# A two-layer hybrid trunk: one wide diagonal at the start, three readerless products before it, and another written-out order

## The chip, the cores and the metric

The kernel runs on one core of a Trainium2 chip, as one program. Its time is device microseconds of one execution; of several runs the median is given. The core has five engines that run their own instruction queues and wait for each other by semaphores: TensorE (PE in the profile; PEld are its weight loads), VectorE (DVE), ScalarE (ACT), GpSimd (POOL) and SyncE (SP), which here only issues DMAs.

## The reference

The input is a sequence of 2048 frames of width 1024. Two layers are applied. Cut to what is computed:

```
for l in range(2):
    shift, scale, gate = split(silu(c) @ w_ada[l] + b_ada[l])
    h = rms_norm(x, norm_g[l]) * (1 + scale) + shift
    gq, gk, gv, glr, gz, dq, dk, dv, dz = split(h @ w_in[l])
    # group A: causal convolution and silu on gq, gk, gv, then gated
    # linear attention in chunks of 64 frames with a decaying state
    # group B: two softmax maps per head, s1 - lam * s2, block-causal
    y = concat(o_gla, o_diff) @ w_out[l]
    x = x + gate * y
```

There are four heads in each group. In group B the queries and keys are normalised, the softmax is over all earlier chunks, and the result of a head is normalised and multiplied by silu of its gate path. Everything is float32.

## The kernel before

The sequence is cut into four units of 512 frames, so there are eight (layer, unit) pairs. For each unit the kernel forms h transposed, as eight tiles of 128 features by 512 frames, each split into a rounded part `hhi` and a remainder `hlo`. A weight block is split the same way into two halves of `w`. A product of two float32 matrices is then three fast products: high by high, high by low and low by high (`mm3T`, `mm3N`). They add up in PSUM banks named `acc` or `sc`. Nine weight items belong to a layer: 0 to 3 the heads of group B, 4 and 5 the inputs of group A, 6 its gate, 7 and 8 the two halves of the output.

For a head of group B and a tile of 128 queries, `scores` forms the products `sc<-Kj,qh`, VectorE writes them negated into `s` with a running minimum, ScalarE takes the exponential, and VectorE combines the two maps. `pv` transposes the map (`tp<-ident,s`), ScalarE copies it, and the products `po<-Vt,s` and `po<-Vj,s` (plain float32, two TensorE instructions each) give the result. Then ScalarE squares it, GpSimd takes the root (`wq`) and VectorE writes `z`. Four tiles of `z` are transposed (`tp<-ident,z`) and split into `oh` and `ol`, with which the output products `acc<-oh,w` and `acc<-ol,w` run in `out_gen`: two halves of eight blocks of twelve products. Block 7 is the last head of group B, blocks 0 to 3 are group A.

The start is written apart, in `start`. It loads c (`cb`), four x tiles (`xt`), the modulation weights of the first layer in eight blocks (`wm`, 1 MB each), x transposed (`xp`) and raw weights. ScalarE sums the squares of each frame; `root` (VectorE `xms`, GpSimd `rs128`) gives the reciprocal roots, one column per 128 frames. They have to lie along the free axis in all partitions. So four VectorE instructions multiply the identity by one column each (tile `dg`, called `t` in the profile), and four products with a matrix of ones spread them over the partitions into one PSUM tile `pb` (tag `tp`). ScalarE copies that to `rsb`. For each block k, VectorE forms shift and scale with two long multiply-and-sum instructions (`wm<-wm,cb`, 1024 wide), then `sv`, `B` and `A`. `make_h` makes `xp`, `hhi` and `hlo`, and 24 products of items 0 and 4 follow.

The order of the work is not the order of this text. `Program` records every instruction (19403), with a cost from `cost` and fixed delays between engines. `order` then lets the engines run in time: each takes the ready instruction with the lowest turn. The turns come from `ORDER`, a packed list of small steps; an instruction's number plus the running sum of the steps is its turn. Written out, the turns are each number from 0 to 19402 once, so they are the place of each instruction in one long list. In the first 45 us of the trace each engine follows it. All instructions are issued from line 358, so the profile's rows are told apart by tile names, not by lines. VectorE's list at the start reads: `xms`, three diagonals, `wm`, `cact`, `wm`, `cact`, the fourth diagonal, `sv`, `B`, six small vectors and `A`, two weight remainders, `xp`.

PSUM has four `acc` buffers and four of tag `tp`, which `sc`, `tp` and `po` share. All DMAs of the kernel are issued by SyncE in list order.

Of the kernel before, what the change touches and what calls it, by code (L numbers as in the profile page):

```python
# [124 lines left out]
class Program:  # L125
# [236 lines left out]
def trunk_kernel(ctx, tc, xl, x, c, ccol, w_ada, w_mod, w_all, w_glr, w_gk, vecs, lam, out):  # L362
    nc = tc.nc
    L = w_all.shape[0]
    NU = xl.shape[0]
    S = NU * UT
# [299 lines left out]
    def start():  # L666
        y = layers[0]
# [24 lines left out]
        V.scalar_tensor_tensor(cb, th, 1.0, cb, op0=ALU.add, op1=ALU.mult)  # L692
        t8 = p_sm.tile([P, KT], F32, tag="t8", name="t8", bufs=1)
# [640 lines left out]
def _layouts(x, c, w_ada, b_ada, norm_g, w_in, conv_w, w_gk, b_gk, gla_norm_g, qn_g, kn_g, lam_q1, lam_k1, lam_q2,  # L1334
# [30 lines left out]
    'NgDTBtVkdU0o_u0@)*wP4Gg?xnTy&zm}NCo>f`bR5Lg(;GG5oe-vs`QnpHJbN;yxvO3Z=cSz0kbTu$e7FgHemw|nzPiYnA+aGqN1s(yIZGnry2LV'
    '8-y&fYT-8%wDsC4|{t8$u>hPKnfGHIALh$i!P4GA9|*9YcCj0o--_V5h?iqD(mfwsiaL#Y}ACr<%ey-W8hDK@z68EuoC-BF0ZNf!rf~)OS93VeMg'
    'v9=QKhXxN|vD1USG!i&b^#rh&)NrxX&SMq_<Fmq3~sLP;2RBcgYKR%LCKWJmzN?+IO=OPUMYZXS(0{VsX-s03uSEWIF^ztgEKWH-lAkC-5GZii*f'
    'aziIqtsqON0cO}eg%_BtF8e{=h}WJ{?z9vj$9ODd?S_(lqkB1foB5O;+q6(rjm(}_HSYC-9N$$V2~Ge^q5GL(9>9kQyr^7G~2;a>j)}q2IQ|nXB='
    'gPJ@wfFx9gfMsh9TL<IBkuf$@c*H&L1DHfaHQV8q`$gPwBuS$?1p+Gy4=F76XcMOG8g7Z4HDDLED`CzC~amx(bZxEh+j2kfsja&;cE#$bPk@R`vz'
# [24 lines left out]
    '@FGaw~vnMgEB)kcEMPA)}s>3+>^>Dz1}Oe26tS$xVR81d1L9yjRZtm7IF_|ME>(i%#XW7{F~{wR}IMQYij+|!~ux{jR&a1d}MYT)^{<mvD+Fd=7e'
# [179 lines left out]
```

## Time and profile before

| | us |
|---|---|
| runs | 2431.47, 2435.93, 2436.93 |
| median | 2435.93 |
| profiled execution, time | 2435.78 |
| profiled execution, span of the core | 2434.1 |
| TensorE busy | 2378.5 |
| VectorE busy | 1823.4 |
| ScalarE busy | 1232.5 |
| GpSimd busy | 125.7 |

The mean granted TensorE clock is 0.995 of full speed. The time is the device's, the span is from the first to the last instruction of the core. Busy shares are means over very different stages. A timeline row gives start, duration, engine, line, operation, output and inputs, shapes, the number of instructions merged into it, and in brackets the idle time of the engine just before with what ended it.

### The profile page before, as it was taken

Reading aid. Unit: us, or ns where it says so; the run is one execution under the profiler, and the core shown is the slowest. Engines: PE = TensorE matmul, PEld = TensorE weight load, DVE = VectorE, ACT = ScalarE, POOL = GpSimd, SP = SyncE. Lnnn points to the kernel's source line nnn. Section 1 sums busy time; section 2 is a strip of 40 time slices with the busy share of each in tenths; the row PEclk is TensorE's granted clock in tenths of the full one; section 3 lists DMA queues with packets and bytes.
Section 4 is the critical chain, followed back from the end, with each engine's and each line's share of the span. In section 5 each row is a group of like instructions: output and inputs, shape, how many; then the busy total and the mean of one; then the engine's idle time right before and its main releaser. Section 6 shows DMA issues by size and latency. Waiting matters only on the chain.

```text
span 2434.1 us, 38504 instructions
## 1 busy us (share of the span) xinstructions
PE 2378.5 (98%) x12895; PEld 1943.7 (80%) x12895; DVE 1823.4 (75%) x5159; ACT 1232.5 (51%) x2726; POOL 125.7 (5%) x400
## 2 busy tenths in 40 slices
PE   7999999999999999999999999999999999999998
PEld 5777787777888778888788777888787887888887
DVE  7878877896578858689965897368764888748883
ACT  3876643555245544445764565245532555324452
POOL 0010000000000000000010010000000000000000
PEclk9999999999999999999999999999999999999999
DMA  8577788786777868678557777676685777776763
GB/s 324 207 267 281 266 316 270 228 278 220 248 233 221 263 212 273 191 222 241 188 205 277 275 257 256 229 236 208 205 271 205 225 221 225 250 234 204 199 211 122
DMA packets 370101, 575.86 MB, mean 237 GB/s; under 512 B 191888, under 2 KB 251760, under 8 KB 366832
## 3 DMA queue, kind: packets, MB, share of 16 engines
q1 hardware_dynamic: 369904, 573.41, 71.4%
q8 instruction: 102, 1.67, 0.3%
q14 instruction: 95, 0.78, 0.1%
HBM read 418.13 MB, written 161.50 MB: 238 GB/s over the span
## 4 chain that ended last, share of the span: by engine, by line
PE 68%; DVE 18%; ACT 5%; DMA 5%; issue 3%; POOL 1%; SPq 0%; POOLq 0%; DVEq 0%; ACTq 0%
PE acc L358 47%; PE sc L358 10%; DVE s L358 8%; PE po L358 7%; PE tp L358 4%; DMA wr<-in_w_ada_dram 2%; DVE t L358 2%; ACT s L358 1%; DVE w L358 1%; DVE xp L358 1%; DVE vN L358 1%; DVE z L358 1%; DMA w<-wd 1%; DVE am L358 1%; DMA s<-ad 1%
## 5 line engine op out<-in xcount | busy, mean ns | idle before, releaser
L358 PE MATMUL acc<-w,hhi 128*128 128x512 f32 x2560 | 841.1, 403 | 5.4 <-ACT hhi L358 2.5
L358 PEld LDWEIGHTS acc<-w,hhi 128*128 128x128 f32 x2560 | 471.9, 189 | 104.2 <-ACT hhi L358 3.9
L358 PE MATMUL acc<-w,hlo 128*128 128x512 f32 x1280 | 497.3, 401 | 0.0
L358 ACT ACTIVATE s<-s,mx 128x128 f32<-128x128 f32 (+15 forms) x256 | 308.3, 1205 | 313.0 <-DVE s L358 188.1
L358 DVE TENSOR_SCALAR_CACHE_REDUCE s<-sc,mx 64x64 f32<-64x64 f32 (+5 forms) x640 | 305.9, 482 | 54.9 <-PE sc L358 35.9
L358 PE MATMUL acc<-oh,w 128*128 128x512 f32 x1024 | 341.8, 401 | 2.6 <-DVE z L358 1.7
L358 PE MATMUL acc<-hhi,w 128*128 128x512 f32 x960 | 315.7, 399 | 1.3 <-ACT ub L358 0.7
L358 PEld LDWEIGHTS acc<-w,hlo 128*128 128x128 f32 x1280 | 240.5, 189 | 47.5 <-DVE hlo L358 1.6
L358 PEld LDWEIGHTS acc<-oh,w 128*128 128x128 f32 x1024 | 191.1, 189 | 43.9 <-DVE z L358 3.9
L358 PEld LDWEIGHTS po<-Vj,s 128*128 128x128 f32 x1536 | 207.2, 196 | 13.8 <-DMA s<-ad 2.6
L358 PE MATMUL po<-Vj,s 128*128 128x128 f32 x1536 | 214.7, 281 | 2.7 <-DMA s<-ad 1.5
L358 PEld LDWEIGHTS acc<-hhi,w 128*128 128x128 f32 x960 | 178.5, 188 | 37.8 <-DVE z L358 1.2
L358 DVE SCALAR_TENSOR_TENSOR s<-s,r 128x512 f32<-128x512 f32 (+2 forms) x320 | 202.2, 666 | 3.1
L358 PE MATMUL acc<-ol,w 128*128 128x512 f32 x512 | 203.3, 400 | 0.0
L358 DVE TENSOR_SCALAR_CACHE_REDUCE s<-sc 128x512 f32<-128x512 f32 (+4 forms) x256 | 158.2, 620 | 55.0 <-PE sc L358 34.9
L358 PE MATMUL acc<-hlo,w 128*128 128x512 f32 x480 | 189.1, 397 | 0.0
L358 PE MATMUL sc<-Kj,qh 128*128 128x512 f32 x384 | 159.1, 417 | 2.4 <-DVE s L358 1.8
L358 PE MATMUL sc<-Kj,ql 128*128 128x512 f32 x384 | 151.6, 399 | 0.0
L358 DVE SCALAR_TENSOR_TENSOR t<-ub,vec,t 128x512 f32<-128x512 f32 x192 | 140.2, 745 | 9.6 <-ACT t L358 8.9
L358 ACT CAST w<-raw 128x512 fp32r<-128x512 f32 x160 | 98.1, 625 | 93.6 <-PE acc L358 74.4
L358 POOL MEMSET s<- 64x64 f32 x256 | 36.9, 144 | 2075.3 <-PE po L358 1309.2
L358 DVE TENSOR_TENSOR w<-raw,w 128x512 fp32r<-128x512 f32 x160 | 108.7, 685 | 33.6 <-ACT w L358 31.8
(183 smaller groups left out, 3617.1 us busy)
## 6 DMA issues: line engine op xcount, KB each, us to landing
w<-wd SPq DMA_DIRECT2D x416, 512.0 KB, 4.3
wd<-w SPq DMA_DIRECT2D x144, 512.0 KB, 5.0
raw<-in_w_all_dram SPq DMA_DIRECT2D x80, 512.0 KB, 5.3
Kj<-kd SPq DMA_DIRECT2D x48, 512.0 KB, 5.9
ad<-s SPq DMA_DIRECT2D x24, 768.0 KB, 4.7
s<-ad SPq DMA_DIRECT2D x24, 768.0 KB, 6.6
wr<-in_w_ada_dram SPq DMA_DIRECT2D x128, 128.0 KB, 4.5
ad<-s SPq DMA_DIRECT2D x32, 512.0 KB, 3.9
```

The costliest lines, as they stand in the source:

```text
L358: getattr(self.engines[e], method)(*[real(a) for a in args], **{k: real(v) for k, v in kw.items()})
```

## The change

Four parts:

- In `start`, the four diagonals become one VectorE instruction over 128 x 4 x 128 elements. Its two inputs are the identity and the four columns of roots, both broadcast. The four products become one 512 wide.
- Ahead of it, three products of the ones matrix with the first 512 columns of `cb` are recorded. Each writes a `tp` tile that nothing reads.
- In `cost`, DMA rows 1024 wide get 480 in place of 350. An instruction on up to 64 partitions and 64 elements gets 216. VectorE's fixed part becomes 81 (130 for one element) in place of 70. A branch for ScalarE instructions of one element stands behind a return for all ScalarE instructions, so it is never reached.
- `ORDER` is another list. 19400 instructions are recorded, and its turns are each number from 0 to 19399 once.

```
         if e == "S":
-            return math.prod(out.shape) * 4 / {64: 208.0, 256: 326.0}.get(out.shape[-1], 350.0)
+            return math.prod(out.shape) * 4 / {64: 208.0, 256: 326.0, D: 480.0}.get(out.shape[-1], 350.0)
...
+        if out.shape[0] <= 64 and n == 64:
+            return 216
...
         if e == "A":
             return 0.834 * n + (45 if psum else 85) + 93 * (scalars + ("accum_out" in kw)) + half
+        if e == "A" and n == 1:
+            return 100 + 93 * ("bias" in kw)
...
-        return (0.52 if fast else 1.042) * n + 70 + 61 * scalars + half + 30 * ("accum_out" in kw)
+        return (0.52 if fast else 1.042) * n + (81 if n > 1 else 130) + 61 * scalars + half + 30 * ("accum_out" in kw)
...
         V.scalar_tensor_tensor(cb, th, 1.0, cb, op0=ALU.add, op1=ALU.mult)
+        for _ in range(3):
+            T.matmul(tp(), ones, cb[:, 0:512], start=True, stop=True)
...
         pb = tp()
-        for t in range(TT):
-            ts_ = slice(t * P, (t + 1) * P)
-            V.tensor_scalar(dg[:, ts_], ident, rs128[:, t:t + 1], None, op0=ALU.mult)
-            T.matmul(pb[:, ts_], ones, dg[:, ts_], start=True, stop=True)
+        V.tensor_tensor(dg.rearrange("p (t n) -> p t n", t=TT), ident.unsqueeze(1).to_broadcast([P, TT, P]),
+                        rs128[:, 0:TT].unsqueeze(2).to_broadcast([P, TT, P]), op=ALU.mult)
+        T.matmul(pb, ones, dg, start=True, stop=True)
         rsb = rs_tile()
...
 ORDER = (
...
```

Compared place by place, 78 of 100 instructions stand within 50 places of the old one. Three parts of the new list matter below.

- VectorE at the start: `cact` twice, `xms`, `wm`, the diagonal, `sv`, `wm`, `A`, a cast of the gate weights, a weight remainder, `B`, a weight remainder, `xp`. SyncE at the start: one x tile, c, one x tile, `cact`, `vec`, two x tiles, `wm`; before, `vec` and `cact` stood behind the first `wm`.
- TensorE at the tail, from the last `po` product: three output products, a transposition of `z`, five output products, the last transposition of `z`, five output products, then block 7. All thirteen are of blocks 1, 2 and 3 of the first half. Before, it was four transpositions of `z` and then block 7.
- In the first layer, unit 0, head 3 and unit 2, head 3 have more products between the scores of a tile and its transpositions than before; unit 3, head 2 has fewer.

More of the change, by code (lines that the diff above doesn't have):

```diff
@@ L1365 @@
[L1365 to L1369, printed above, removed]
@@ new lines @@
+    '6nc)Y3woiQz#W;@rW~(ndgA7_vn(3iZxbn@^eI~4BJc($x)$4T@e2(Aat^)f@-=^%gQ@6o-7{Y4NH}(dAL-mt1m+TWVM2dn*oB8o+T$8WImaNTu9'
+    'T3iDmNEo<~7NW35)fUuYuOE2!ml%g+k98?!)G30ZP;PtoB5L0%ynDxXi6y4${y+Hy|zA@t8CI&8cshhyjyI}>Es=_WGzh3UkBjnRA4@$<ysSp-in'
+    'gYDtAcd_peLW-sAb~<1OPH_YYOsRCU1+iqMG@NhME8jT~h%dSx#q=f&Vff-&-1vJ$o%JUz`%A6x<-6i;XUXaMEK+WB2HPPjBcg*He*HK>@DOV{bX'
+    'L)U`d>_!D7kqr{-sQQg5wx%r<@z%SHFs^SN3QCTp(od#lW$fWhs_9p*`e4DocfvT<lX_N1?6M>*0ozVNdlL;=I=Nwk?L{FL~MX*rABpWknIKSu=^'
+    'ks__?b5$4HazYU$YWoV|hv(QklnpCp$RQS1*69OF~-c5|3tj+JE-|&J9Iu>yNxCa`7z`X8N;lYA(dVO*qoyuCTM>p4jf652C$`Wccn`A(3cGhD9#'
@@ new lines @@
+    'P-c^m|TGN%7=#PXrs=qUcm?qcIbHQ^B#mRW&%GNU^R6DuB2YL+#Me*osp`!S9@S#GS^mpAmZ=i;KqT|TgDsxj8=A1cz_<fCY%IjaXgvQg@_F|nGi'
+    '0ED=oLn`kgIrqR;Om7!i>q0OI?XmOM;3_Ln@fqhb=Yn;`7E5Vm(9b5*3|_UZEZi^bpG5Z%ycbw~wxZ)i+zW9yR4AwvtRyuYzs3pC7`2}e`?+<LSh'
+    'a%B<H@MrXRNau^EAJ^5u&HBBsOJMmj>ye;hLNdte7b~fQYv)8zNdKYoMXixB2OfyNiPt2jG?9=4Rqid{T55=C)D|{*Bm-yc0}VZ@rXaqe--HwL<@'
+    '&P5){cRglrufBcZ<e|WlnF9y-BZrScrLDc_4PPBl3Q($xa;q5gT8j+kS@qj}qskxx23l1|B_ghw%ints^FmyQmwy02!|d*EO?hpipkY0ul|{>zv{'
+    'xxXBk0;Ge+`SU?|)&b@3s7c?NM_H+9$lA!Ri82uW0y-gDUX0q2zhO}^UvN60|63Zr#BI0`rB`wa!Ck9MR5fbH4Yc&G~_<WDL*gl-@@no^i!B4;Tp'
@@ new lines @@
+    'yMYJRFHu&f%UIW44%r?^j?4jZa&~o-i`XlFq?7<5*NN&6Z`l-&?1G!6{~%P{lnXDNR0D^4mUdY;R1qPdF>vgjfgeh9!+~*By|QJcO3^52m<c|3DQ'
+    'yY%l19b{dbw<>Vsi;$f?CWA!WO|oCplpEK~T={h6uM6cx$?tQ@c;6;2324XeeFHzamgZU4|zVMEj;#k-ayILW2Ml7_Blt+uEu42PP*28Q6I*Yx2$'
+    'Ab2Fbb4J0R3<PYQDS1`Ak)+yO`NHOZ6N-<SkF=5i7z`T5oQVkb`>AV^j9~9f32o9EEDzEAceB@zhDH$;fGa)0%p%)Dr-Lz2Y6cr-XM<e;xc9*~Dl'
+    'n<(M>>Iq+zfcOxf1?~Th(bQkAyHo4JKymxskp3Zp_UBsa}g^H$)LeT{+yRcKx)*J#PtJSPrr@gbk`&c;9tK?o4JOYu^}P`Woh&kTVms8-jiCm;NX'
+    '(Jc>J))6Hl7HkIaG)WvabRe{`TdzOW_%e`+s>U)$b)-axSi{iKX(n{*VM#X}+yI({gyA55_f(ded?~}Kmv~<WsI>a8meJ5k`g(q^>-U@MIcdrT{u'
@@ new lines @@
+    '6@3<GSw;l8_fdCH$W*az45-Y^|M^4bN#6lRtB=pauUlr_nXpVt^nZG&&-EHpxPKB6LDcGco4K-OlX@V$CfjhZj7$deAZ2Y>7ARFohxs{_<b5I<fN'
+    'Kn3ftY3OZC}FiR=y8TjdP9a{_cW8u6CUcm2m2lYj?xUo{-0`tlUHU>A>?TXKQUt}+poFLTbbf{GG;TD72ZvP93$9g@o91#Q8}sSd{O&7{y+5iEzJ'
+    'nv+}84|uFtY&z?LVmwOfgfpiSrXzwHC0y;yTGR0)ikIrR<R0WPzif19al`PxpgTffAhf2r!eq+=N`2}<mARTB83@Fs2J%=P&qyQd-mOEHk`pjS>9'
+    'VGnvS)t?!KGS@(W-CkF}q;FpH50vp~%&X2CM1(%$ZJ`HSPnE><6WjVGinQqn&E^;F5wQT7<e{ib%bfASlj~X@>Jd*yO|xCoClH?F~u@DkOLjwEeX'
+    '+(2l0>$rYP`z^%w8q8QdYWY`1gIb)lsD<|t0YWW#L7ANL2evfznr#J}WPD=Yitqlvr^Wy6`-7Ywp;((CrvGi+zCi2ngES2!E1#Rq=b&H#d#j=V8n'
@@ new lines @@
+    '`VS!9A58{hA&%3udVQMrXAWHv~o_9UZ)-@RJkc~7AN=MZpE=CKlsUJ2^2xi5a$MX9<)}9dpZN{nG_>lM~9rvLmvrRSBBs=RQ8~~i4rl-m9?8}E6O'
+    '^!jrNWw0Fk{-Qt=xxOw1Az6R!kFL_WO@N?N8_Fn=sLq5u7R{V&Y+O1G*jT_}rzcR=Ea`LxN>shn6JpfwqcZep{;F10l=XX#O9_d6Ddxv4ALdhxFv'
+    '=#w!P8iwk8gPUb|va;1@gmv)E5Yj6TK4b8|o$Jj^8`sdH2wSi>sa_xvBDItVp~x&JLi4&|JAE2*OgRITf~UD#M6=3B+0W?sS<Ok0MqrKlQE>&V6D'
+    'u_VKH%Hp&UbQ4FYxOzL@f1(4cMi<()o;ejNOTrQ!=?GBa$WYd;s-LV2ZU;ljPgdXU8AJfGXMkTvs9c!;hC);uRT(MQ^^AITe#Il%*X?1ISYL#H1c'
+    'GP4f!9jr?R9<*7;<aw6O-VZ(AY^>=G6BIF+AC}#*XXIg_ips5R-I>|!|a!4W(cg`NO<5{H94d<%8Wc}9y>HBep+r^4oap_#-rVwO{Bpm-${*#~+W'
@@ new lines @@
+    '}LTC0Ct4p;+R|yGmL7`qV<a(kx{o|1!KVhW^XTIk>niFqHX8UZf&c@6IdM-B&C{mTJiO(e$&xt&>E*+<*zJmjsv3d5qn6Xr8pbkechVvZ#_*s%z-'
+    'g8IXutA)$TgVD;AnL%X~?Pl%#>%bYV1~tksbs<TttQu5hCcNnmpz?nAI6X=|T{39idFkkj;IT~Wl&<M$;|n+vj?ey;|%po5()=fA!XeWd!Zd1zqB'
+    'W{Ry`{}E}FdGS;<LVm}hbpzlDVrNjo6oVk)rzAPL!cI=na|G34fVQR~Og%{k_TVEJwoyFMa5`Fi3^3KOp8zc<cArXHx*@0~b};m9p6h1Uy7%P_>;'
+    '}4vO41R0l*+t8-u9KnG0>KKAqHM;DvkM}Fg>bAZOC|bEiCqtg$y*uU*4eO<7LNURhQ=4p>xBC^U;)TrF@fXkB^C!Cy6YpvkFSw$_fQhrK3cp#9X)'
+    '}f*{zqP0HDL>jIzVbn~e|$V8T&uz3>qgd)<V1ol!gC35MYs?qJPhCV1bQOn9jQqg9VjYsxq${JM}*e<a<FcvkwS4za8p;heLOM*tXPY92+X7s)Q4'
@@ new lines @@
+    'iQ-IeHPF;Z(}$AIc)`|@!j16!S6;ba}9Zt*T|exmXB!xGO+xQi!ZscbP2k~+m<mDk${VxQehtz<C|c;n&bi*5F9W;z<K7Kx9n}FBSs>bSa~g;$9&'
+    'B8Ph+|aQ%ZW3or@|7ymK8|?q{De-@{(ii7Tn?2Ys*;<7`Ebb|pqQX2E#as6OM+t-L%ZMsV%5K~*!B-@g3#k9SQocbsE{^~%3EI;bl-vH-mLb#lRH'
+    '(*&=I*}mi5f83vD!;kT+V10sU*{f$KzL&7Kk#vB~vmq_teN`o){h1~X9t4dU5x_QWSteQLez7+kaeL7c-SY7T4^Lc`fR|=weWYAlEW!9SWUu_<AN'
+    'oi2kbz*}GP`CynhhjbegYZ3KK!f4{tds6w3#W^a+ms~om_@g2=%Yr`v9>YQKvgHu9Li=hcrmjuvx0X>{{c|YFvHUY_vl=^Pqior&a|w9ikV3DDl1'
+    'rkbGh|vFZ8j>DZ{CKNDj>0vCRvd`-43gVPW;UE8?5TJ?sf^t9XK3gH?PD|egK#eX9{%jkWQGa${B81D?&N?18B`h+^r?B>O6tqb-iI5J<_+Ak^?m'
@@ L1552 @@
+    'Iz_iqjlCOJPe*nwaIxCR8n(ZSYukDX{^#F`bKkTG`Ol>q+IhJaIs(kN@#Az8c_D?2rwb>hAHi}(g=PU<I0(6PRn{!vMwp|v^DYWsSr|xXsh{`EbP'
+    'd|LOntxluFrxw-L@F<Pg&E6#CJ4To;S?s+>YwJ|bEmo*g5z9C0f>&`^1z?GsM(L;pRj)U#G_)-Gy+j5OJG%i*Iehe*dnAjpVe6nl_bqXNEWrvr^A'
+    '{=OxRxy?W>4^@e2U(2JDb{=KMrK!N~<B(g_30c@2n1wi}uQjztNQ`RtCX)<z$FT~Br0cgKV3ckv00000jjZC?5lq&<00Fs-0g$f(Y}L33vBYQl0s'
+    'sI200dcD'
 )
```

350 lines of the change are left out of this document (163 added, 187 removed).

## The prediction

> **What bounds the kernel now.** I read the page first: the busy shares, then the chain that ended last.
>
> ```profile
> span 2434.1 us, 38504 instructions
> PE 2378.5 (98%) x12895; PEld 1943.7 (80%) x12895; DVE 1823.4 (75%) x5159; ACT 1232.5 (51%) x2726; POOL 125.7 (5%) x400
> ...
> PE 68%; DVE 18%; ACT 5%; DMA 5%; issue 3%; POOL 1%; SPq 0%; POOLq 0%; DVEq 0%; ACTq 0%
> ```
>
> TensorE is idle for only 2434.1 - 2378.5 = 55.6 us, and it is two thirds of the chain. The change takes no real work from it. So the time can move in three ways only: TensorE starts its stream earlier or later, its idle spells grow or shrink, or it runs for more or less time at half clock. The profiled execution took 2435.78 us by the times, 0.15 us under the median 2435.93, so a sum made against it stands for the median. Its span is 1.7 us shorter than its time, and I keep that difference.
>
> Next I read the timeline of the start and the busy table of the stages where the granted clock is below 1.00 (columns after the stage: TensorE, its weight loads, VectorE, ScalarE, GpSimd, granted clock, DMA share, GB/s).
>
> ```profile
> 7.71 1.22 DVE L358 SCALAR_TENSOR_TENSOR cb<-th,cb 128x1024 f32<-128x1024 f32 x1 [5.06 <-ACT th L358]
> 10.60 1.06 ACT L358 ACTIVATE xt<-xt 128x1024 f32<-128x1024 f32 x1
> 11.78 0.17 DVE L358 TENSOR_SCALAR xms<-xss 128x4 f32<-128x4 f32 x1 [2.84 <-ACT xt L358]
> 12.03 1.03 POOL L358 TENSOR_TENSOR rs<-xms,mhalf 128x4 f32<-128x4 f32 x1 [10.32 <-DVE xms L358]
> 13.09 0.68 DVE L358 TENSOR_SCALAR t<-ident,rs 128x128 f32<-128x128 f32 x3 [1.15 <-POOL rs L358]
> 13.44 1.22 PE L358 MATMUL tp<-t,ones 128*128 128x128 f32 x4 [13.44 <-DVE t L358]
> 13.69 1.22 DVE L358 SCALAR_TENSOR_TENSOR wm<-wm,cb 128x1024 f32<-128x1024 f32 x1
> 16.13 0.28 DVE L358 TENSOR_SCALAR t<-ident,rs 128x128 f32<-128x128 f32 x1
> 17.72 0.58 ACT L358 COPY rsb<-tp 128x512 f32<-128x512 f32 x1 [0.62 <-PE tp L358]
> 18.34 0.75 DVE L358 SCALAR_TENSOR_TENSOR xp<-xp,A,rsb 128x512 f32<-128x512 f32 x1
> 20.02 2.08 PE L358 MATMUL acc<-w,hhi 128*128 128x512 f32 x4 [2.33 <-ACT hhi L358]
> 24.02 1.05 PE L358 MATMUL acc<-w,hhi 128*128 128x512 f32 x2
> 24.88 0.63 PE L358 MATMUL acc<-w,hlo 128*128 128x512 f32 x1
> 26.60 0.85 PE L358 MATMUL sc<-hhi,w 128*128 128x512 f32 x3
> 27.29 0.39 PE L358 MATMUL sc<-hlo,w 128*128 128x512 f32 x1
> ```
>
> ```profile
> 20.00:60.00 40.00, 39.98 (x165) 32.74 (x166) 37.29 (x86) 12.55 (x20) 0.67 (x5) 1.00 0.80 315
> 104.00:108.00 4.00, 3.17 (x12) 1.95 (x10) 3.84 (x15) 2.25 (x8) 1.01 (x3) 0.52 0.65 227
> 220.00:240.00 20.00, 16.51 (x81) 12.34 (x81) 19.17 (x76) 14.63 (x43) 2.60 (x10) 0.93 0.89 323
> 240.00:260.00 20.00, 19.82 (x90) 14.98 (x89) 20.00 (x40) 10.68 (x20) 0.73 (x2) 0.90 0.42 149
> 860.00:880.00 20.00, 17.46 (x100) 14.46 (x99) 16.86 (x54) 12.42 (x35) 1.67 (x7) 0.91 0.74 208
> 2400.00:2420.00 20.00, 17.70 (x76) 14.25 (x75) 4.10 (x6) 1.35 (x4) 0.54 (x1) 0.91 0.54 189
> ```
>
> Two things are to be seen. The first 128x512 products start 0.43 us apart ((24.88-24.02)/2) and from 26.60 on 0.23 us apart ((27.29-26.60)/3), so TensorE runs its first six microseconds at half speed. And from 20 to 60 us both TensorE (39.98 of 40) and VectorE (37.29 of 40) are nearly full. Half speed returns at three later places and at the tail.
>
> **The tail.** In the timeline after the last attention block TensorE has nothing left but the chain of that block:
>
> ```profile
> 2399.66 1.06 PE L358 MATMUL po<-Vt,s 128*128 128x128 f32 x8
> 2402.56 0.33 PE L358 MATMUL tp<-ident,z 128*128 128x128 f32 x1 [1.52 <-DVE z L358]
> 2403.67 1.22 PE L358 MATMUL acc<-oh,w 128*128 128x512 f32 x4 [0.78 <-ACT oh L358]
> 2405.11 0.63 PE L358 MATMUL acc<-oh,w 128*128 128x512 f32 x1
> 2405.54 0.63 PE L358 MATMUL acc<-ol,w 128*128 128x512 f32 x1
> 2411.83 0.39 PE L358 MATMUL acc<-ol,w 128*128 128x512 f32 x1
> 2412.06 0.61 PE L358 MATMUL acc<-oh,w 128*128 128x512 f32 x2
> 2412.51 0.39 PE L358 MATMUL acc<-ol,w 128*128 128x512 f32 x1
> ```
>
> It waits 1.52 and 0.78 us and then runs at 0.43 us a product (2405.11 to 2405.54) instead of 0.227 ((2412.51-2411.83)/3). The old order leaves only three transpositions behind the last po product. The new order leaves products of the first half of the output (its blocks 1, 2 and 3): 8 of them and one transposition before the last z transposition, 5 more before the first product that needs its result. The chain from the end of po (2399.66 + 1.06 = 2400.72) to 2402.56 takes 1.84 us; the cover is 8 x 0.227 + 0.11 = 1.92 us. The next link, 2402.56 to 2403.67, takes 1.11 us; the cover is 5 x 0.227 = 1.13 us. Both just reach. So 2.30 us of waits go, and with them the half clock: (1 - 0.91) x 20 = 1.8 us, all of it lost time, since TensorE has work without a break from 2403.67 on. **Term: -4.1 us.** Bounds: 0 if the held products are missed where they stood before, -4.1 otherwise. I take the full value, since the attention rows before it are covered by transpositions and po products in both orders.
>
> **The start.** The three readerless products read cb, which is complete at 7.71 + 1.22 = 8.93 us. No such fp32 128x512 product is in the trace. The 128-wide pairs bound it: eight po instructions (four products) span 1.06 us at full clock, so a four times wider product is about 1 us; at half speed it is about 1.8 us. Three take 3 to 5.4 us, until 12 to 14.3 us. TensorE is idle until 13.44 now, and its next product must wait for the diagonal, so they cost nothing unless that product were ready before 14.3.
>
> The diagonal is one 128x512 VectorE instruction in place of four of 128x128 (0.28 us each, 0.23 apart in the row of three). The nearest row is another 128x512 two-operand instruction without PSUM:
>
> ```profile
> L358 DVE TENSOR_TENSOR w<-raw,w 128x512 fp32r<-128x512 f32 x160 | 108.7, 685 | 33.6 <-ACT w L358 31.8 <-DMA wd<-w 0.9
> ```
>
> 0.69 us against 4 x 0.23 = 0.92: 0.2 us less, bounds 0.5 less to 0.5 more for the two broadcast inputs. One wide product instead of four narrow ones is equal work. What matters is place. Before, the fourth diagonal stands behind two modulation products and runs at 16.13, so rsb is ready at 18.30 and xp starts at 18.34: the root ends last. In the new order one modulation product (1.22 us) stands ahead of the whole diagonal and the other behind it. The loads of vec and cact now go ahead of the third and fourth x load; they are 74 KB against 512 KB for each x load, whose squares follow each other every 1.3 us, so xms moves from 11.78 to about 12.0. The first modulation weights land about two such loads later (1 MB), near 13.4; then 1.22 us of product, 0.69 us of diagonal: 15.3. The wide product and the copy (0.58) make rsb ready at 17 to 17.8. But VectorE then has the second modulation product, the vector A, a gate weight cast and two weight remainders (0.69 each) ahead of xp: 15.3 + 1.22 + 0.3 + 0.25 + 1.38 + 0.1 = 18.5. So xp starts at 18.5 against 18.34 and the first product at about 20.1 against 20.02. The wait moves from the root to VectorE. Bounds: 1.7 us earlier (xp right behind A) to 1.8 later (the gate weights' VectorE work of about that size is now ahead of the first products). **Term: 0.**
>
> Does the clock stay up? Here idle time of only 1.67 us was followed by half speed:
>
> ```profile
> 103.74 0.41 PE L358 MATMUL tp<-ident,s 128*128 128x128 f32 x2 [1.67 <-DVE s L358]
> ```
>
> and the row 104 to 108 grants 0.52. Between the wide product's end (about 16.5 to 17.2) and 20.1 lie about 3 us, so I expect the first products cold again. The Trainium skill's "TensorE: Matmul & The Clock Gate", in its Part 1, says otherwise: a window of about 3.4 us of activity releases the clock and a whole idle window of that length takes it back. By that rule three products release it and 3 us would not always take it back; the sum would then gain the cold start. This is the first rival below.
>
> **The new order elsewhere.** The list gives every instruction another place, most within 50 of the old one. What I can price is TensorE work between a result and its user, counted at 0.227 us a product. At three known waits it differs much.
>
> ```profile
> 237.30 0.47 PE L358 MATMUL tp<-ident,z 128*128 128x128 f32 x1 [2.07 <-DVE z L358]
> 867.23 0.71 PE L358 MATMUL po<-Vt,s 128*128 128x128 f32 x4 [1.14 <-ACT s L358]
> ```
>
> At 237.30 (unit 0, head 3) the cover of the third z grows from 1.1 to 8.8 us, and that from the last scores to their first transposition from 1.4 to 9.9. Idle 2.07 plus clock (0.07 + 0.10) x 20 = 3.4 make 5.5 us at most. But VectorE is full there (19.17 and 20.00 of 20), so only the VectorE work that the new order puts behind counts: about 1.7 us, by the counted durations. **Term: -1.7** (0 to -5.5). At 867.23 (unit 2, head 3) the cover grows from 2.8 to 5.1 us; idle 1.14 plus (1 - 0.91) x 20 = 1.8 is 2.9 at most. VectorE has room, but a chain of about 5.4 us would still not be quite covered. **Term: -1.5** (0 to -2.9). Against it: in unit 3 of the first layer, head 2, the cover of the last tile falls from 8.1 to 4.8 us. That chain is one reduction, the exponential and four combining instructions:
>
> ```profile
> L358 ACT ACTIVATE s<-s,mx 128x2048 f32<-128x2048 f32 x16 | 32.1, 2007 | 14.8 <-DVE s L358 14.6
> L358 DVE SCALAR_TENSOR_TENSOR s<-s,r 128x512 f32<-128x512 f32 x224 | 160.5, 747 | 2.1
> ```
>
> 2.0 + 4 x 0.7 + about 1.6 = 6.4 us, so up to 1.6 us is new idle; in unit 0, head 0, one z cover falls to 1.6, below the 1.84 of the tail. **Term: +1.0** (0 to +1.9). All other waits I take as redrawn with mean 0 and about 4 us either way. The wait at 103.74 has the same instructions around it in both orders and stays. The corrected model figures cost nothing on the chip; they act only through the order.
>
> **Sum.** -4.1 + 0 - 1.7 - 1.5 + 1.0 = -6.3: 2435.8 - 6.3 = **2429.5 us**.
>
> **The rivals.**
> 1. The clock stays up through the start, or the two middle spells pay in full. A warm start is worth about 5.7 us x half = 2.8 us (20.02 to about 25.7). For it: the readerless products fill 3 us or more. Against: 3 us idle behind them, and VectorE nearly full until 60 us, so a faster TensorE only waits. The full middle spells are worth 3.8 + 1.4 = 5.2 more than I took. 2429.5 - 2.8 = 2426.7; with all, 2421.5.
> 2. The order only moves the idle spells. For it: TensorE's work is the same and the held products were filling other waits. Then only about half of the tail remains and the waits elsewhere come back: 2435.8 - 2 = 2434, within 2431.1 to 2440.
> 3. Slower: VectorE sets the pace in the first 40 us. By the counted durations the new order has 2.7 us more VectorE work ahead of TensorE's first 20 us of products (gate weights drawn forward). If TensorE then waits over about 1.5 us for the second or third h tile, a cold spell like that at 103.74 follows: 1.67 idle and about 5 us of clock (104 to 108 alone: 0.48 x 4 = 1.9). 2435.8 - 4.1 + 2.7 + 1.7 + 5 = 2441. Against it: from 20 to 48 us the chain is TensorE's own, and by 50 us of products VectorE's lead is gone.
> 4. The chip doesn't follow the list. In the trace of before it does, as far as the start and tail show, so this goes into rival 2.
>
> **Chances.** Forecast case (2426.8 to 2431.0) 0.42; rival 1 0.17; rival 2 0.27; rival 3 0.14. About 0.2% (4.9 us) is what a measurement of this kernel tells from no change. Faster by more: 0.42 + 0.17 = 0.59, less 0.01 for the edge: 0.58; within: 0.28; slower: 0.14. The range leaves out the full sum of rival 1's edge and rival 3's far part: 2420 to 2441; the likeliest case's own range is 2426 to 2433.
>
> **What would show it.** After: no wait of over 0.5 us between the last po and the last products, and granted clock 1.00 over the last 30 us; if not, the first term is wrong. One wide diagonal near 15 us behind one modulation product, xp near 18.5 and the first product near 20, spaced 0.43; spacing 0.23 at once means rival 1. Waits of TensorE in the 20 to 60 us stage mean rival 3. Clock 1.00 in 220 to 260 and 860 to 880 shows the middle terms; TensorE idle in all well under 55.6 us the whole. If idle is the same and the time too, it is rival 2.

## The result, and the profile after

The kernel after takes 2416.87 us (median of four runs, 2414.58 to 2419.43) against 2434.77 for the kernel before (2431.47 to 2436.93): a ratio of 0.9928, 95% interval [0.9911, 0.9945], or 17.9 us less. The forecast was 2429.5 within 2420 to 2441. So the direction was right and the size was about a third of what came. The profiled execution took 2415.17 us, its span is 21.0 us shorter than that of before.

The page of the kernel after, its span, busy shares and chain:

```profile
span 2413.1 us, 38502 instructions
PE 2369.6 (98%) x12895; PEld 1944.9 (81%) x12895; DVE 1825.1 (76%) x5156; ACT 1235.0 (51%) x2726; POOL 121.1 (5%) x400
...
PE 56%; DVE 4%; ACT 2%; DMA 2%; issue 1%; POOL 0%; SPq 0%; DVEq 0%; ACTq 0%; POOLq 0%
```

TensorE's busy time fell by 8.9 us although the readerless products add 5.5. To see real work alone I leave out the start. The busy table from 20 us to the end, of before and then of after (the columns after the stage are TensorE, weight loads, VectorE, ScalarE, GpSimd, granted clock, DMA share, GB/s):

```profile
20.00:2434.10 2414.10, 2376.08 (x12887) 1941.84 (x12887) 1813.76 (x5120) 1221.98 (x2709) 123.64 (x391) 1.00 0.72 236
```

```profile
20.00:2413.10 2393.10, 2362.74 (x12887) 1942.36 (x12887) 1815.40 (x5118) 1225.30 (x2711) 118.98 (x391) 1.00 0.72 238
```

The same 12887 instructions take 13.3 us less busy time, and idle time falls from 38.0 to 30.4 (2414.10 - 2376.08; 2393.10 - 2362.74). The granted clock explains part of the busy time. The stages of the kernel after that answer to those shown of before:

```profile
20.00:60.00 40.00, 38.48 (x160) 30.68 (x161) 38.84 (x90) 12.76 (x21) 0.76 (x5) 0.96 0.81 319
104.00:108.00 4.00, 2.96 (x10) 2.17 (x11) 3.81 (x17) 2.21 (x7) 0.17 (x2) 0.62 0.63 214
220.00:240.00 20.00, 16.43 (x82) 13.32 (x81) 18.83 (x70) 13.62 (x39) 2.52 (x9) 0.95 0.84 300
240.00:260.00 20.00, 19.75 (x100) 15.04 (x99) 19.84 (x44) 11.50 (x23) 0.83 (x3) 0.96 0.54 196
860.00:880.00 20.00, 18.96 (x111) 15.51 (x111) 14.78 (x50) 10.38 (x26) 1.30 (x5) 1.00 0.71 211
2400.00:2410.00 10.00, 9.42 (x41) 7.14 (x39) 2.65 (x4) 0.00 (x0) 0.00 (x0) 1.00 0.51 188
```

The dip at 860 and the one at the tail are gone (0.91 to 1.00), those at 220 and 240 are smaller, the one at 104 stays. Over all stages of 20 us the missing clock is 12.2 us before and 8.6 after. The row of before hides 2.8 us more: it grants 1.00 from 20 to 60 while the products there are 0.43 us apart until 25.7, because its trace holds no record of the clock ahead of 25.62. So 15.0 became 8.6.

The start of the kernel after, from the timeline:

```profile
9.13 1.22 DVE L362 SCALAR_TENSOR_TENSOR cb<-th,cb 128x1024 f32<-128x1024 f32 x1
10.40 5.49 PE L362 MATMUL tp<-cb,ones 128*128 128x512 f32 x6 [10.40 <-DVE cb L362]
12.44 0.17 DVE L362 TENSOR_SCALAR xms<-xss 128x4 f32<-128x4 f32 x1 [1.81 <-ACT xt L362]
13.74 1.23 DVE L362 SCALAR_TENSOR_TENSOR wm<-wm,cb 128x1024 f32<-128x1024 f32 x1 [1.14 <-DMA wm<-in_w_mod_dram]
14.89 0.69 DVE L362 TENSOR_TENSOR t<-ident,rs 128x512 f32<-128x512 f32 x1
15.68 1.34 PE L362 MATMUL tp<-t,ones 128*128 128x512 f32 x2
18.26 0.73 DVE L362 SCALAR_TENSOR_TENSOR xp<-xp,A,rsb 128x512 f32<-128x512 f32 x1
19.80 1.22 PE L362 MATMUL acc<-w,hhi 128*128 128x512 f32 x2 [2.78 <-ACT hhi L362]
20.82 1.91 PE L362 MATMUL sc<-hhi,w 128*128 128x512 f32 x4
23.22 0.62 PE L362 MATMUL sc<-hhi,w 128*128 128x512 f32 x2
28.05 0.50 PE L362 MATMUL sc<-hhi,w 128*128 128x512 f32 x1 [1.02 <-ACT hhi L362]
```

The three products take 1.8 us each, the wide diagonal 0.69, xp starts at 18.26 and the first product at 19.80, all close to the forecast. From 23.22 on products are 0.23 us apart, 2.5 us earlier than before. But at 28.05 TensorE waits 1.02 us for the next h tile, so nothing of it is left.

### The profile page after: what moved, and what is told of

Same layout as the page of the kernel before. It is cut to its first block, busy times and chain, and to the rows that moved or that the text cites. A ratio compares the mean times of both kernels' runs of the same rounds, so it can differ in the third digit from the quotient of the medians.

```text
span 2413.1 us, 38502 instructions
## 1 busy us (share of the span) xinstructions
PE 2369.6 (98%) x12895; PEld 1944.9 (81%) x12895; DVE 1825.1 (76%) x5156; ACT 1235.0 (51%) x2726; POOL 121.1 (5%) x400
## 4 chain that ended last, share of the span: by engine, by line
PE 56%; DVE 4%; ACT 2%; DMA 2%; issue 1%; POOL 0%; SPq 0%; DVEq 0%; ACTq 0%; POOLq 0%
PE acc L362 37%; PE sc L362 8%; PE po L362 7%; PE tp L362 3%; DVE s L362 2%; DMA w<-wd 1%; DVE t L362 1%; ACT la L362 0%; ACT s L362 0%; ACT L362 0%; DMA out_dram<-rt 0%; DMA xp<-xd 0%; DVE ql L362 0%; DMA wr<-in_w_ada_dram 0%; DVE w L362 0%
## 5 line engine op out<-in xcount | busy, mean ns | idle before, releaser
L362 PE MATMUL acc<-w,hlo 128*128 128x512 f32 x1280 | 490.1, 399 | 0.2 <-DVE hlo L362 0.2
L362 ACT ACTIVATE s<-s,mx 128x896 f32<-128x896 f32 (+15 forms) x256 | 308.4, 1205 | 344.0 <-DVE s L362 201.9
L362 PE MATMUL acc<-oh,w 128*128 128x512 f32 x1024 | 330.4, 396 | 1.6 <-DVE z L362 1.1
L362 DVE SCALAR_TENSOR_TENSOR s<-s,r 128x512 f32<-128x512 f32 (+3 forms) x320 | 202.6, 666 | 2.7
```

Source lines behind the costliest of these rows:

```text
L362: getattr(self.engines[e], method)(*[real(a) for a in args], **{k: real(v) for k, v in kw.items()})
```

## The experiments

In both kernels the issued order is the list itself, on each engine. So an experiment can graft one list into the other. All kernels below but the two with exchanged figures have this edit, which alone changes nothing, and a list of their own:

```
-        return self.order(turn.tolist())[0]
+        return np.argsort(turn).tolist()
```

To compare traces inside, I count TensorE's instructions from the first product of h on, each weighted by its width (transpositions and plain float32 products twice: 128 columns of them take about 0.11 us, 512 of the others 0.23), and take for each kernel the time at which it has done as much as the kernel before at a given time. The table gives the difference in us (below zero: ahead of the kernel before), one profiled execution each.

| at (us of before) | after | list only | first layer new | second layer new | tail new | old figures | TensorE swapped | VectorE, ScalarE swapped |
|---|---|---|---|---|---|---|---|---|
| 45 | 1.1 | 1.3 | 1.1 | -1.5 | -0.2 | 3.0 | 2.5 | 3.7 |
| 366 | -2.4 | -1.8 | -1.2 | -2.6 | 0.2 | -1.1 | 2.8 | 3.4 |
| 884 | -6.8 | -6.6 | -3.7 | -4.1 | -0.1 | -1.4 | 8.2 | 10.0 |
| 1197 | -8.1 | -7.1 | -4.7 | -3.5 | -0.1 | -2.0 | 7.8 | 10.2 |
| 1980 | -14.6 | -14.8 | -4.9 | -7.9 | -2.5 | -5.1 | 6.4 | 10.4 |
| 2398 | -17.1 | -16.8 | -4.7 | -10.9 | -3.2 | -5.3 | 4.9 | 10.2 |
| 2411 | -21.0 | -20.7 | -4.8 | -14.9 | -7.2 | -9.3 | 1.0 | 6.2 |

How far one curve can be read: the kernel with only a new tail has the old order until 2343 and still drifts by up to 3.1 us, and the one with the second layer new stands 4.1 us ahead at 884, where its order is still the old one. In another kernel (one transposition moved, below) a stretch of 100 us without any edit lost 2 us to the kernel after, with two waits of 0.66 and 0.35 us for weights (`DMA w<-wd`). So differences under about 4 us in this table are one execution's own.

### Where along the kernel the gain arises

**The first layer in the new order, the second in the old.** ORDER: the first 9800 places of the new list, then the old order.

> The kernel after, whose instructions follow its own list up to place 9800 (about 1197 us, the end of the first layer) and the old list's order behind it. Theory S (the gain is a sum of local waits, removed stage by stage): at equal TensorE work the kernel after stands 9.9 us ahead of the kernel before at 1197 us, so this kernel is 9.9 us faster than before (2425 us) and runs at the old pace behind. Theory W (the gain comes from the start parts, the readerless products and the wide diagonal, and all later work only starts earlier or meets other waits): the whole 18 us, 2417. Theory T (only the removed tail is real, the rest is redrawn with mean 0, as I had predicted): 0, 2435. Theory L (a list works only as a whole): less than 4 us, over 2431.

Measured: 2427.24, ratio 0.9975 [0.9965, 0.9986], 6.1 us faster. **The second layer in the new order**, on the kernel before with its own start:

> The kernel before with its own start (four narrow diagonals, no readerless products) and its old list up to about 1197 us, and the new list's order behind it. Theory S: the second layer with the tail accounts for what is left of the whole, 18 to 21 minus 9.9, so 8 to 11 us faster than before (2424 to 2427). Theory W: 0 (2435). Theory T: the tail alone, 4.1 us (2431). Theory L: less than 4 us.

Measured: 2423.45, ratio 0.9958 [0.9945, 0.9970], 10.2 us faster. The two halves together make 16.3 of the 17.9 us. W falls: a kernel with the old start has most of the gain. T falls: the tail cannot be 10 us. S holds in sum, though the first layer gave less than its 9.9 (the table has 8.1 there for the kernel after).

**The tail alone.**

> The kernel before with its old list up to about 2343 us and the new list's order only in the last 3 per cent. My prediction's first term: 4.1 us faster (2430.7), no wait of over 0.5 us between the last po product and the last products, granted clock 1.00 over the last 30 us. Theory S by the aligned traces: 4 to 5 us. Theory W: 0. Theory T: 4.1.

Measured: 2430.03, ratio 0.9992 [0.9983, 1.0002]: 1.9 us, with an interval from 4.1 faster to 0.5 slower. In its trace there is no TensorE wait over 0.5 us after 2353.5, and from 2398 to 2411 it gains 4.0 us in the table. The kernels after, list only, and both with swapped queues gain 3.9 to 4.0 there too. The trace shows the term of 4.1; the times of this one kernel don't confirm it.

**The list alone**, without the wide diagonal and the readerless products:

> The kernel before with its own instructions (four narrow diagonals in one row where the wide one stands, four narrow products, no readerless products) in the new list's order throughout. Theory S: the list is all of it, and at the first product the two kernels stand within 0.2 us, so 16 to 18 us faster than before (2417 to 2419), within 2 us of the kernel after. Theory W: 0 to 4 us (the tail). The first 20 products then show the old spacing of 0.43 us until about 2.8 us later than in the kernel after.

Measured: 2418.73, ratio 0.9942 [0.9928, 0.9956], 14.1 us faster. The interval meets that of the kernel after: the other parts are worth between nothing and some 3 us.

**The kernel after without its readerless products:**

```
-        for _ in range(3):
-            T.matmul(tp(), ones, cb[:, 0:512], start=True, stop=True)
```

> The kernel after without its three readerless products (nothing reads what is left out); all else in the same order. Theory S, and my prediction's start term of 0: the first products are spaced 0.43 us until about 2.8 us later than in the kernel after (25.7 instead of about 23), but the kernel after waits for the next h tiles there anyway, so from 45 us on the two stand level and the time is that of the kernel after (2417, within 2 us). Theory W2 (the earlier end of the half clock is worth its 2.8 us to the end): 2420, 2.8 us slower than the kernel after.

Measured: 2417.97, ratio 0.9937 [0.9925, 0.9949], as the kernel after. But the expected longer cold start did not come. Its timeline:

```profile
15.36 2.07 PE L362 MATMUL tp<-t,ones 128*128 128x512 f32 x2 [15.36 <-DVE t L362]
19.65 1.22 PE L362 MATMUL acc<-w,hhi 128*128 128x512 f32 x2 [2.22 <-ACT hhi L362]
20.67 1.91 PE L362 MATMUL sc<-hhi,w 128*128 128x512 f32 x4
22.38 0.84 PE L362 MATMUL sc<-hlo,w 128*128 128x512 f32 x2
23.06 0.62 PE L362 MATMUL sc<-hhi,w 128*128 128x512 f32 x2
```

Products are 0.43 us apart until 22.38 and 0.34 and 0.23 behind it, no later than with the readerless products. So these products did not bring the earlier end of half speed, and they are worth nothing here. Both theories had that step wrong. Two stretches of the busy table of the kernel after show what became of them:

```profile
16.19:19.60 3.41, 0.83 (x2) 0.00 (x0) 3.37 (x10) 1.16 (x2) 0.00 (x0) 1.00 1.03 413
19.60:23.01 3.41, 3.21 (x8) 2.54 (x9) 3.07 (x7) 1.80 (x4) 0.00 (x0) 0.50 1.02 424
```

They did bring the full clock, at 16.19. But TensorE was busy for only 0.83 of the next 3.41 us, and at 19.60, 0.20 us before the first product, the clock fell back to half for another 3.41 us. Over all profiled executions of these experiments and of the two kernels, the half speed at the start ends between 22.4 and 25.6 us in the ten with readerless products (in one it comes back from 29.3 to 32.7) and between 22.7 and 25.9 in the nine without.

**The middle alone**, between 142 and 366 us, and the same with its end at 466:

> The kernel before with the new list's order only between about 142 and 366 us (unit 0, heads 1 to 3 of the first layer, with the wait at 237.30 that I priced at 1.7 us of at most 5.5). Theory S: at equal TensorE work the kernel after gains 3.7 us there, the kernel before with the new list throughout 4.4, so 3.7 to 4.4 us faster than before and the stretch 220 to 260 at a granted clock of about 0.95 each instead of 0.93 and 0.90. My prediction: 1.7. Theory L (a graft loses the gain at its seams): 0.

> As the kernel with the new list only in the middle, but the new order runs on to about 466 us before the old one returns. That kernel stood 3.4 us ahead at 366 us and lost 4.7 at its second seam (a wait of 2.61 us for am at 377, which neither parent has). Theory S: with the seam elsewhere the gain of the middle stays, 3 to 6 us faster than before (the kernels with the new list stand 3.2 to 5.9 us ahead at 440 to 560). Theory L (each seam costs what the graft gains): 0 again.

Measured: 1.0009 [0.9999, 1.0019] and 0.9993 [0.9984, 1.0001]: no gain in either. The first stands 3.6 us ahead at 366 and 1.2 behind at 440, the second 6.6 ahead at 440 and 1.6 at 560. The timelines of the two at their seams:

```profile
376.55 0.58 PE L358 MATMUL sc<-ones,am 128*128 128x1 f32 x4 [2.61 <-DVE am L358]
```

```profile
477.17 0.99 PE L358 MATMUL sc<-ones,am 128*128 128x1 f32 x4 [3.05 <-DVE am L358]
```

`am` is a long VectorE chain for the next layer's modulation. In both, TensorE asks for it too early where the old order returns, and a cold spell follows (granted clock 0.91 from 370 to 390 in the first, 0.83 from 470 to 490 in the second). So L is right for short grafts: the gain of a stretch is real within it, and a seam can take it back. My claim that it adds up stage by stage holds for the two layers, not for any piece.

### Whether list and figures belong together

**The kernel after with the cost figures of before** (its list kept; `order` as it was), **and the kernel before with the figures of after**:

> The kernel after with the cost figures of before; list and instructions are those of after. The planner takes the lowest turn among what its figures call ready, so with other figures it issues another order: 43 of 100 instructions stand at another place of the whole, 2 of 100 by more than 10 places; on TensorE's own queue 7 of 100, on VectorE's 22 of 100. Theory F (list and figures belong together, and small swaps on VectorE's queue bring back the waits): most of the gain goes, 2427 or more. Theory S with order counted as a coarse thing (cover of products between a result and its user): swaps of a few places cost nothing, 2417 to 2421.

> The kernel before with the cost figures of after; list and instructions are those of before. 48 of 100 instructions are issued at another place, 1.5 of 100 by more than 10. Theory F: slower than before, by 5 us or more (over 2439). Theory S with coarse order: within 4 us of before. Theory N (the corrected figures alone let the planner put ready work where the chip has it ready): faster than before by 5 us or more.

Measured: 2428.84, ratio 0.9984 [0.9975, 0.9993], so about 12 to 14 of the 18 us are gone; and 2435.99, ratio 1.0013 [1.0004, 1.0022], 3 us slower than before. F holds for the first and only in sign for the second (3 us, not 5). N falls: the corrected figures alone make nothing faster. What a displaced instruction costs can be seen at one place. The timeline of the kernel after, then of the one with the old figures:

```profile
863.73 2.04 PE L362 MATMUL po<-Vj,s 128*128 128x128 f32 x16
865.65 0.44 PE L362 MATMUL tp<-ident,ae 128*128 128x128 f32 x2
```

```profile
867.21 0.33 PE L358 MATMUL tp<-ident,ae 128*128 128x128 f32 x1 [1.77 <-ACT ae L358]
867.37 3.55 PE L358 MATMUL po<-Vj,s 128*128 128x128 f32 x16
```

One transposition has slipped ahead of 16 ready instructions. It waits 1.77 us for ScalarE, all 16 wait with it, and they then run at half speed.

**That one transposition moved in the kernel after, nothing else:**

> The kernel after with one TensorE instruction moved: the first transposition of ae (unit 2, head 3) stands ahead of the eight po<-Vj,s products (16 TensorE instructions) at 863.73 instead of behind them, as it does in the kernel with the old figures. All other queues are those of after. Theory F in its local form (an instruction at the head of TensorE's queue that is not ready stops all ready ones behind it, and the clock drops behind the wait): that place alone costs what it cost with the old figures, a wait of 1.77 us for ScalarE's ae and 3.55 instead of 2.04 us for the 16 instructions, 3.3 us in all, visible in the aligned traces between 857 and 884, and 2420 in time. Rival R (the next wait, for z at 867.24, falls away instead, and the work behind it has slack): under 1 us, 2417.

```profile
868.07 0.33 PE L362 MATMUL tp<-ident,ae 128*128 128x128 f32 x1 [1.76 <-ACT ae L362]
868.24 2.05 PE L362 MATMUL po<-Vj,s 128*128 128x128 f32 x16
```

Measured: 2421.00, ratio 0.9939 [0.9926, 0.9953]; against 0.9928 that is 2.7 us, which the intervals don't resolve. The wait is there again, 1.76 us, but this time the clock stays up (2.05 for the 16). Within this stretch the trace loses 1.6 us to the kernel after, not 3.3: neither theory's number.

**Eleven products moved ahead at two waits that remain; and the same with the old start:**

> The kernel after with eleven TensorE instructions moved at two of its remaining waits: six products ahead of the four transpositions of s at 494.94 (idle 1.03), five ahead of the two scores at 1997.23 (idle 1.03). If a wait is a matter of what stands at the head of the queue, both fall under 0.2 us and about 2 us go (2415); if the late chain only becomes later for its next user, the idle comes back within the next 20 us and the time stays (2417).

> The kernel before, start and old list up to about 142 us, then the new list with the two moves. At 142 us all kernels with the new start stand 1 to 2.5 us behind the old one at equal TensorE work (waits of 1.02 and more for the next h tiles at 28 us). Theory S: 1.7 us for the start and 2 for the moves off the kernel after, 2413. If the start is hidden and the moves are worth nothing: 2417. Theory L (the seam at 142 costs something): over 2417.

Measured: 2416.78, ratio 0.9928 [0.9915, 0.9940], and 2416.85, ratio 0.9921 [0.9908, 0.9935]. Neither is better than the kernel after. The waits of the first, from the timeline:

```profile
495.65 0.66 PE L362 MATMUL tp<-ident,s 128*128 128x128 f32 x4 [0.31 <-ACT t L362]
496.61 0.55 PE L362 MATMUL tp<-ident,rw 128*128 128x128 f32 x3 [0.30 <-ACT vN L362]
500.41 0.33 PE L362 MATMUL tp<-ident,rs 128*128 128x128 f32 x1 [1.00 <-POOL rs L362]
...
1999.80 0.50 PE L362 MATMUL sc<-Kj,qh 128*128 128x512 f32 x1 [0.49 <-DVE s L362]
```

The wait of 1.03 us at 494.94 fell to 0.31, and 0.30 and 1.00 came behind it. That at 1997 fell to none, and 0.49 came at the next scores. The chain is as late as before; its next user finds it so.

**One engine's queue at a time in the order of the old figures.** The other queues stay as in the kernel after.

> The kernel after, with TensorE's queue alone in the order of the kernel with the old figures (7 of 100 TensorE instructions at another place); the other four queues are those of after. The whole swap cost 13.6 us (ratio 0.9984 against 0.9928). Theory Q (what counts is which instruction stands at the head of TensorE's queue): most of it, 9 to 14 us, so 2426 to 2431. Theory V (the waits come from VectorE and ScalarE working in a worse order): under 4 us, under 2421.

> The kernel after, with the queues of VectorE (22 of 100 instructions at another place) and ScalarE (7 of 100) in the order of the kernel with the old figures; TensorE, GpSimd and the DMAs as in after. Theory Q: under 4 us of the 13.6 are lost, under 2421. Theory V: 9 to 14, 2426 to 2431.

> As the kernel with VectorE's and ScalarE's queues from the old figures, with the DMA queue and GpSimd's from there too; only TensorE's is that of after. Theory Q: under 4 us lost, under 2421. Theory V: 9 to 14, 2426 to 2431. If this kernel loses 5 us or more beyond the one without the DMA queue, it is the order of the weight and score DMAs that costs (the waits for w in the traces).

Measured: 0.9995 [0.9986, 1.0004], 1.0052 [1.0038, 1.0066] and 1.0037 [1.0024, 1.0049]: 15, 27 and 24 us slower than the kernel after by the medians. Neither Q nor V: each part alone costs more than all together (12 to 14). The engines' orders fit each other, and what is harmful is that one is changed without the others. The DMA order adds no loss (the third is not slower than the second). At the place of the transposition, the second of them shows one such case. Its rows of VectorE and TensorE, and that of VectorE in the kernel after:

```profile
879.02 1.30 DVE L362 STREAM_TRANSPOSE s<-s 128x512 f32<-128x512 f32 x2
880.25 0.18 DVE L362 CAST wglr<-t 128x128 fp32r<-128x128 f32 x1
...
882.30 0.29 DVE L362 SCALAR_TENSOR_TENSOR z<-th,acc 128x128 f32<-128x128 f32 x1
...
882.64 0.80 PE L362 MATMUL acc<-oh,w 128*128 128x512 f32 x1 [3.99 <-DVE z L362]
```

```profile
866.91 0.28 DVE L362 SCALAR_TENSOR_TENSOR z<-th,acc 128x128 f32<-128x128 f32 x1
```

In the swapped VectorE order this `z` stands behind two transpositions of `s` and a row of gate weight casts. In the kernel after it stands ahead of them. TensorE's queue, which is that of the kernel after, meets it 3.99 us too early.

### The part that is neither wait nor clock

Of the 13.3 us less busy time the clock explains 6.4. In the timeline TensorE's rows are bursts of short instructions (transpositions and plain float32 products, nearly all 128 wide) between stretches of the wide fast products. The two lists differ in how often TensorE changes between the two kinds: 1481 times before, 1241 after. I had not counted this. **More changes, and fewer:**

> The kernel after with one 128x512 product moved from behind a burst of short TensorE instructions (transpositions and po products, 128 wide) into its middle, at 219 places; so TensorE changes between 512-wide and 128-wide instructions 1679 times instead of 1241 (the kernel before: 1481). All other queues as in after; a product comes earlier and half a burst 0.23 us later. Theory C (each change costs TensorE some 0.02 us, as a fit of the row starts over stretches without waits gives, 0.018 for the kernel before and 0.022 for after; then 240 fewer changes are worth about 5 us of the gain, a term that my prediction did not have): 438 changes more cost 8 to 9 us, about 2425, without more waits. Rival M (changes cost nothing: bursts of 1, 2, 3 and 4 transpositions cost 0.11, 0.22, 0.32 and 0.44 us with the longer product behind them): 2417, or as much more as the new waits in the trace add up to.

> The kernel after with one or two 128x512 products that stood between two bursts moved ahead of the first, at 100 places: 1095 changes instead of 1241; all other queues as in after. Theory C: 146 fewer changes are worth 2.9 us, 2414, if the 0.23 to 0.45 us by which the first burst comes later is covered. Rival M: 2417, or slower by the waits that the later bursts bring.

Measured: 2423.97, ratio 0.9954 [0.9942, 0.9967], and 2422.38, ratio 0.9948 [0.9935, 0.9962]. The busy tables from 20 us on, of the first and of the second:

```profile
20.00:2422.10 2402.10, 2371.51 (x12887) 1941.33 (x12887) 1816.32 (x5118) 1225.17 (x2711) 119.22 (x391) 1.00 0.73 237
```

```profile
20.00:2419.90 2399.90, 2364.61 (x12887) 1944.46 (x12886) 1816.25 (x5117) 1223.62 (x2711) 118.77 (x391) 1.00 0.73 237
```

With 438 more changes TensorE is busy 8.8 us longer (2371.51 - 2362.74) and idle as long as in the kernel after (30.6 against 30.4). 1.6 us of it is clock (10.2 us missing over all stages against 8.6), so a change costs (8.8 - 1.6)/438 = 0.016 us, a little under what C said, and it is no wait; M falls here. With 146 fewer the busy time did not fall but rose by 1.9 us (2364.61), so C's saving was not seen, and idle time rose to 35.3: the later bursts made their users late, for which M has a place. So merging did not pay, and this kernel is some 5 us slower.

Whether two executions can carry that price, the others tell. For all 19 profiled executions (these experiments with the two kernels) I set the busy time from 30 us on, less the missing clock, against the number of changes of the issued order. A straight line has 0.014 us per change (correlation 0.80); before and the split bursts lie highest, both at 2354.2. The seven with 1241 changes scatter from 2346.2 to 2351.2, so a saving of 146 changes, 2.3 us, can't be seen in one execution.

## Why the prediction was wrong

The account of the 21.0 us in the profiled spans, from 20 us on, beside the forecast (the medians differ by 17.9, so some 3 us of it belong to these two executions):

| | idle | clock | sum | forecast |
|---|---|---|---|---|
| tail | -2.3 | -1.8 | -4.1 | -4.1 |
| 20 to 60 | +1.5 | -1.2 | +0.3 | 0 |
| 220 to 260 | +0.2 | -1.6 | -1.4 | -1.7 |
| 860 to 880 | -1.5 | -1.8 | -3.3 | -1.5 |
| everywhere else | -5.5 | 0.0 | -5.5 | 0, and +1.0 |
| 240 fewer changes, estimated at 0.016 each | | | -3.8 | none |
| not assigned | | | -3.2 | none |

- **The tail** was right in each part: no wait behind the last po product, granted clock 1.00.
- **The start, 0**, was right at the first product (19.80 for about 20.1), and right in sum because two things cancelled that the term did not hold. Rival 3's wait for the next h tile came (1.02 us at 28.05, 1.5 us of idle time in all until 60), and not at a cost of 5. Rival 1's earlier end of the cold spell came (1.2 us), but not by the readerless products, as the kernel without them shows.
- **The wait at 237.30** was right in size by luck, for a reason I did not give. The wait for z went, and a longer one came a moment later, here from the timeline of the kernel after:

```profile
238.01 2.06 PE L362 MATMUL acc<-w,hhi 128*128 128x512 f32 x4 [3.55 <-ACT hhi L362]
```

The idle time stayed and only the clock gained. I had asked what the removed wait costs, not what is late next.

- **The wait at 867.23** was under-sized: "VectorE has room, but a chain of about 5.4 us would still not be quite covered". It was covered, and the next wait, for z, shrank as well (the timeline of before, then of after):

```profile
874.99 0.50 PE L358 MATMUL acc<-oh,w 128*128 128x512 f32 x1 [0.81 <-DVE z L358]
```

```profile
867.24 0.50 PE L362 MATMUL acc<-oh,w 128*128 128x512 f32 x1 [0.17 <-DVE z L362]
```

With both went the half clock.

- **The new cover loss, +1.0**, is not to be seen as a wait of its own.
- **The step that failed** is "All other waits I take as redrawn with mean 0 and about 4 us either way". Elsewhere the idle time fell by 5.5. It is not the scatter of single executions: from 60 us to the last po product TensorE is idle for 23.5 to 28.8 us (mean 25.8) in the five with the new order throughout (the kernel after, list only, without the readerless products, one transposition and eleven products moved), and for 29.4 to 33.0 (mean 31.3) in the four with the old one but for a middle or the tail. Between the means that is 5.5 us, against 6.6 in this pair. Which waits make it up is not taken apart here. The new order is no random redraw of the old one. The planner makes one order of all engines from list and figures, and it fits the engines to each other: with the old figures most of the gain goes, and with the order of one or two engines alone exchanged all of it or more. That the new list and its figures belong together is shown. How much of the gain another list could have had with the old figures is open, since no such list was made; the new figures with the old list are 0.13% slower.
- **The other failed step** is "So the time can move in three ways only". There is a fourth: TensorE's own instructions stand closer or wider by their neighbours. The number of changes could have been counted in the two lists before the run, and a price stood in the kernel itself: `order` adds 32 ns at each change to a narrow instruction, which is 16 ns per change. The split bursts show that price for added changes. That 240 fewer gave 3.8 us, about as much as the tail, is an estimate from it, and the merged bursts did not confirm it. Another 3.2 us of busy time are neither clock nor changes at this price; what they are stays open.

Rival 2 (2434) and rival 4 fall. Rival 1 with all its terms gave 2421.5, the nearest, for reasons that were mostly not the ones at work.

## What to carry to other kernels

When a whole order is replaced, price it as a whole: count what differs over the full lists (TensorE's changes between narrow and wide instructions, the place of each result against that of its user on the other engine) before taking the unpriced rest as zero. A wait that is covered gives what the next late result leaves of it. Where the program plans its own order, its plan is a forecast too: the last time that `order` plans is 2399.0 us in the kernel before and 2386.1 in the kernel after, each by its own figures, and 12.9 us less is nearer to the 17.9 measured than the sum of 6.3 was. And orders of several engines that were made together have to be kept together: an improvement to one queue alone can cost more than the whole change gains.

## What the hardware showed that was not expected

- The same wait costs differently from one execution to the next. 1.77 us of idle time was followed by 16 instructions in 3.55 us, 1.76 us at the same place of the other kernel by the same 16 in 2.05. The granted clock of the traces shows the difference. In all 19 profiled executions it is either 1.00 or 0.50, it changes only at marks 3.41 us apart, and a half spell lasts 3.41, 6.83, 10.24 or 13.65 us. Here are the stretches between such marks around the wait, of the kernel with the old figures and of the one with the transposition moved:

```profile
864.05:867.46 3.41, 1.64 (x14) 0.88 (x11) 1.65 (x4) 3.40 (x6) 0.14 (x1) 1.00 1.08 312
867.47:870.87 3.40, 3.40 (x18) 3.40 (x17) 3.32 (x8) 0.17 (x1) 0.00 (x0) 0.50 0.21 77
```

```profile
863.23:866.64 3.41, 2.63 (x18) 1.67 (x18) 2.21 (x7) 3.38 (x5) 0.14 (x1) 1.00 1.07 337
866.64:870.05 3.41, 1.98 (x17) 1.98 (x18) 1.80 (x4) 1.86 (x5) 0.00 (x0) 1.00 0.49 190
870.06:873.47 3.41, 3.23 (x19) 2.61 (x19) 2.82 (x12) 2.65 (x11) 0.68 (x2) 1.00 0.01 2
```

The wait of 1.77 us lay whole between two marks, TensorE was busy for 0.48 of that stretch, and half speed followed. The wait of 1.76 us was divided by a mark, the two stretches were busy for 0.77 and 0.58, and the clock stayed. Over all 19 executions there are 40 stretches at full clock in which TensorE was busy for less than 0.45, and half speed followed each of them. It followed none of those busy for more than 0.63, and 29 of the 53 in between. The Trainium skill's "TensorE: Matmul & The Clock Gate", Part 1, says that the window over which activity is judged is free-running and doesn't start with the kernel. The marks agree with that: the first is at 25.62 us in the kernel before and at 16.19 in the kernel after, 9.43 us apart, which is no whole number of steps. They don't agree with its table, by which half speed needs an idle window of about 3.4 us: a wait of 1.77 us was enough.
- For the same reason the end of the cold start moves: 22.8 us without the readerless products, 23.0 with them, 25.6 before. A gain there can't be read from one execution.
- An added change between 128-wide and 512-wide TensorE instructions costs about 0.016 us, seen only in sums: in single rows, given to 0.01 us, it is lost.
